# A hybrid decoder layer on one core: output projection, post-norm and gate kept in step order, summed in place, with the norm sums placed between matmuls

## The chip, the core and the metric

The kernel runs on one core of a Trainium2 chip. The metric is the device time of one execution in microseconds (us); of three runs of the kernel before the median is 534.99 (534.62 to 535.94). All stages are matmuls in fp32 accuracy: each fp32 operand is split into a high part, rounded by ScalarE (ACT), and the rest, formed by VectorE (DVE), and each product is three matmuls (high by high, low by high, high by low).

## The reference

T = D = 1024. Of the layer the last part matters here:

```
mixed = concat(ssm_out, attn_out) @ w_out          # (T, 1024)
h     = x + rms_norm(mixed, post_norm_g)           # norm over the 1024 features
gate  = sigmoid(h @ pl_w_gate + pl_b_gate)
out   = h + gate * (p @ pl_w_proj)                 # p has 256 features
```

Before it come a pre-norm, the input projection, an S5 state-space branch (`ssm_out`) and a sliding-window attention branch (`attn_out`).

## The kernel before, in words

Features lie on the 128 partitions, tokens along the free dimension, so a tile `m` of 128 output features is 128 x 1024, held in two PSUM banks of 512 columns ("halves", `HALF`). A token has two orders. In time order column t is token t. In step order a column is j * 128 + c for token 8c + j: eight steps j of 128 chunks c. The state-space branch works in step order, the attention branch in time order.

The last part of the program, from L955 on:

- The first half of the output projection (4 of 8 contraction tiles, those of the state-space branch) has been run during attention; its result stands in two tiles `mixed` in step order.
- `per_layer(m)` (L957) is `p @ pl_w_proj` for tile m: 12 matmuls from `pt` (p, transposed and split), copied out by ACT into `pls`. Tiles 0 to 2 are run ahead of the projection.
- `a_hi`, `a_lo` (L973 to L977) are the split of the attention output `q_f`, one instruction per block of 128 tokens on ACT and one on DVE. The last block comes from the last attention unit, whose DVE instruction L799 (`q_f<-ps,z_att`) gates it.
- The loop L981 runs the second half of the output projection, 24 matmuls a tile. DVE adds each half to `mixed` (L993) and writes `total` in time order, which makes the operand `mixed` strided; ACT squares it (L994); DVE gathers `sumsq` (L998, and by halves for the last tile, L996).
- `over_partitions` (L125) sums `sumsq` over the partitions with eight one-column matmuls (each shows as two). `row_rstd` (L132) makes the reciprocal root of it with 12 small DVE instructions and spreads it over the partitions with eight transposes (L151) and two ACT copies (`postb`).
- `make_h(k)` (L1007) forms tile k of h: DVE scales (L1015) and adds x (L1016), ACT and DVE split (L1018, L1019).
- The gate: tiles 0, 1, 2 are run together over k (18 matmuls per k, L1053 to L1058), as h comes; tiles 3 to 7 after that, one by one. The weights of tile 2 go into a tile `w_2` of their own (L1047 to L1051), loaded once `make_h(1)` has run.

Order: a scheduler sets the order on ACT, DVE and the DMA queue (SP) by priorities and modelled times; PE's order in the blocks `manual_schedule` is as written. Every engine runs its own instructions strictly in that order. Space: `t16` gives seven slots of 16 KB per partition, `t4` four of 4 KB, `w_st` two for weights as they land, `w_hi` and `w_lo` four each for the split. A new tile in a slot waits until the old one was read for the last time. `run` on the host lays out the inputs; that is not part of the time.

Of the kernel before, what the change touches and what calls it, by code (L numbers as in the profile page):

```python
# [20 lines left out]
P = 128  # L21
# [30 lines left out]


def layer_kernel(
    tc, x_in, xT, pT, w_in, w_glu, w_out, w_gate, w_proj, vecs, sinks,
    lam_re, lam_im, log_step, bc, ssm_d, out,
):
    nc = tc.nc
# [2 lines left out]
    with ExitStack() as top:  # L61
# [13 lines left out]
        def t16(shape, dt, name):  # L75
            return mp.tile(shape, dt, name=name, tag="t16", bufs=7)

        def t4(shape, dt, name):
            return mp.tile(shape, dt, name=name, tag="t4", bufs=BUFS["t4"])
# [26 lines left out]
                w.append((hi, lo))  # L106
            return w

        def product(ps, w, act, ks, first=True, last=True):

            ah, al = act
            for n, (kw, ka) in enumerate(ks):
                wh, wl = (t[:, kw % 4, :] for t in w[kw // 4])
                f, l = first and n == 0, last and n == len(ks) - 1
                for h, o in enumerate(ps):
                    PE.matmul(o, lhsT=wh, rhs=ah(ka, h), start=f, stop=False)  # L116
                for h, o in enumerate(ps):
                    PE.matmul(o, lhsT=wh, rhs=al(ka, h), start=False, stop=False)  # L118
                for h, o in enumerate(ps):
                    PE.matmul(o, lhsT=wl, rhs=ah(ka, h), start=False, stop=l)  # L120

        def by_half(tiles, n=4):
            return lambda k, h: tiles[k // n][:, k % n, h * HALF : (h + 1) * HALF]

        def over_partitions(sumsq):  # L125
            ps = bank("w")
            for t in range(8):
                PE.matmul(ps[:, t : t + 1], lhsT=sumsq[:, t * P : (t + 1) * P],
                          rhs=ones_col, start=True, stop=True)
            return ps[:, 0:8]  # L130

        def row_rstd(sums, name, between):  # L132
# [819 lines left out]
                n += 1  # L952
        run_pieces(n, end)

        pls = []  # L955

        def per_layer(m):  # L957
            w = load_split(w_proj[m], 2)
            ps = psum_pair("tab" if m % 3 == 1 else "mm")
            product(ps, w, (by_half([pt[:, 0]]), by_half([pt[:, 1]])), [(0, 0), (1, 1)])  # L960
# [10 lines left out]
        for m in range(3):  # L971
            per_layer(m)
        a_hi = t16([P, 4, T], F32R, "a_hi")  # L973
        a_lo = t16([P, 4, T], F32R, "a_lo")
        for b in range(NB):
            qs = slice(b * P, (b + 1) * P)
            split_to(a_hi[:, :, qs], a_lo[:, :, qs], q_f[:, :, qs])  # L977
        total = [t16([P, 4, T], F32, "total") for _ in range(2)]
        sumsq = t4([P, T], F32, "sumsq2")
        aact = (by_half([a_hi]), by_half([a_lo]))  # L980
        for m in range(KT):  # L981
            w = load_split(w_out[m][:, 4:KT], 4)
            ps = psum_pair("tab" if m % 3 == 1 else "mm")
            product(ps, w, aact, [(k, k) for k in range(4)])
            sq = sumsq if m == 0 else t4([P, T], F32, "sq2")
            for h, o in enumerate(ps):
                hs = slice(h * HALF, (h + 1) * HALF)
                mix = total[m // 4][:, m % 4, hs]

                def chunks(t):  # L990
                    return t.rearrange("p (c j) -> p c j", j=CH)
                steps = mixed[m // 4][:, m % 4, :].rearrange("p (j c) -> p c j", j=CH)[:, 64 * h : 64 * h + 64, :]
# [12 lines left out]
        lows = []

        def make_h(k):  # L1007
            x2 = t4([P, T], F32, "x2")
            nc.sync.dma_start(out=x2, in_=xT[k * P : (k + 1) * P, :])
# [20 lines left out]
            nc.sync.dma_start(out=out[m * P : (m + 1) * P, hs], in_=t)  # L1030

        with tc.manual_schedule(engines={mybir.EngineType.PE}):
            def some(lo, hi):
                for m in range(lo, hi):
                    per_layer(m)
# [7 lines left out]
            w_first = [load_split(w_gate[m], KT) for m in range(2)]  # L1043
            with tc.high_priority(offset=2 * AHEAD):
                made = make_h(1)

            w2 = t16([P, 2, KT, P], F32R, "w_2")  # L1047
            w_first.append([(w2[:, 0, 4 * i : 4 * i + 4], w2[:, 1, 4 * i : 4 * i + 4]) for i in range(2)])
            with tc.issue_after(made.ins):
                for i in range(2):  # L1050
                    load_part(*w_first[2][i], w_gate[2], slice(4 * i, 4 * i + 4))  # L1051
# [79 lines left out]
```

## Time and profile before

| | us |
|---|---|
| median of three runs | 534.99 |
| the profiled execution | 535.14 |
| its span | 533.4 |
| PE busy in the span | 517.3 (97%) |
| DVE, ACT busy | 379.8, 214.2 |

PE is the engine of matmuls, PEld its weight loads, SPq the issue of DMAs by SyncE. "Busy" of PE counts any running matmul, a one-column one too; "idle before" in brackets is the time in which the engine waited, and what released it. The 1.7 us between the span and the time of the execution lie around the program.

### The profile page before, as it was taken

Reading aid. Unit: us, or ns where it says so; the run is one execution under the profiler, and the core shown is the slowest. Engines: PE = TensorE matmul, PEld = TensorE weight load, DVE = VectorE, ACT = ScalarE, POOL = GpSimd, SP = SyncE. Lnnn points to the kernel's source line nnn. Section 1 sums busy time; section 2 is a strip of 40 time slices with the busy share of each in tenths; the row PEclk is TensorE's granted clock in tenths of the full one; section 3 lists DMA queues with packets and bytes.
Section 4 is the critical chain, followed back from the end, with each engine's and each line's share of the span. In section 5 each row is a group of like instructions: output and inputs, shape, how many; then the busy total and the mean of one; then the engine's idle time right before and its main releaser. Section 6 shows DMA issues by size and latency. Waiting matters only on the chain.

```text
span 533.4 us, 7319 instructions
## 1 busy us (share of the span) xinstructions
PE 517.3 (97%) x2472; PEld 410.4 (77%) x2472; DVE 379.8 (71%) x864; ACT 214.2 (40%) x443; POOL 8.6 (2%) x37
## 2 busy tenths in 40 slices
PE   7999999999999999999899999999999998999996
PEld 5888887888888888886445767777788886888886
DVE  4778997989889898654699667666467679736232
ACT  5676120311122322233775656667332373223121
POOL 1000000000000000010000000000000000000000
PEclk9999999899999999999999999999999989999999
DMA  7961638344443434559575122101111165124112
GB/s 268 372 233 60 217 93 196 95 128 121 122 117 97 120 95 117 176 145 252 169 213 190 47 60 60 30 22 39 61 49 30 67 218 174 65 80 172 66 39 79
DMA packets 48053, 66.10 MB, mean 124 GB/s; under 512 B 10128, under 2 KB 25232, under 8 KB 48016
## 3 DMA queue, kind: packets, MB, share of 16 engines
q1 hardware_dynamic: 46736, 63.54, 38.6%
q10 hardware_dynamic: 1280, 2.10, 1.5%
q8 instruction: 19, 0.31, 0.3%
q14 instruction: 18, 0.15, 0.1%
HBM read 44.12 MB, written 11.01 MB: 103 GB/s over the span
## 4 chain that ended last, share of the span: by engine, by line
PE 80%; DVE 9%; DMA 7%; SPq 1%; issue 1%; ACT 1%; ACTq 0%; DVEq 0%
PE ps_mm L118 18%; PE ps_mm L116 18%; PE ps_mm L120 18%; PE ps_tab L120 4%; PE ps_tab L116 4%; PE ps_tab L118 4%; PE ps_mm L866 3%; DMA y_all<-y_dr 2%; PE ps_w L794 2%; PE ps_y L794 2%; PE ps_tab L737 1%; PE ps_tab L738 1%; PE ps_y L594 1%; PE ps_w L520 1%; DVE e L314 1%
## 5 line engine op out<-in xcount | busy, mean ns | idle before, releaser
L88 ACT ACTIVATE w_hi<-w_st 128x512 fp32r<-128x512 f32 (+1 forms) x68 | 41.2, 606 | 132.3 <-PE ps_mm L118 80.6
L116 PE MATMUL ps_mm<-x_hi,w_hi 128*128 128x512 f32 x272 | 86.3, 399 | 2.3 <-ACT x_hi L178 1.7
L118 PE MATMUL ps_mm<-x_lo,w_hi 128*128 128x512 f32 x272 | 87.7, 399 | 0.0
L120 PE MATMUL ps_mm<-x_hi,w_lo 128*128 128x512 f32 x272 | 87.4, 398 | 0.0
L89 DVE TENSOR_TENSOR w_lo<-w_st,w_hi 128x512 fp32r<-128x512 f32 (+1 forms) x68 | 44.8, 659 | 38.7 <-ACT w_hi L88 32.4
L116 PEld LDWEIGHTS ps_mm<-x_hi,w_hi 128*128 128x128 f32 x272 | 51.3, 191 | 13.6 <-ACT x_hi L178 2.2
L118 PEld LDWEIGHTS ps_mm<-x_lo,w_hi 128*128 128x128 f32 x272 | 51.6, 191 | 10.5
L120 PEld LDWEIGHTS ps_mm<-x_hi,w_lo 128*128 128x128 f32 x272 | 51.2, 191 | 10.2 <-DVE w_lo L89 0.3
L118 PE MATMUL ps_mm<-h_lo,w_hi 128*128 128x512 f32 (+1 forms) x96 | 30.8, 380 | 0.0
L116 PE MATMUL ps_mm<-h_hi,w_hi 128*128 128x512 f32 (+1 forms) x96 | 30.8, 380 | 0.0
L120 PE MATMUL ps_mm<-h_hi,w_lo 128*128 128x512 f32 (+1 forms) x96 | 30.7, 380 | 0.0
L761 ACT ACTIVATE sc<-sc,mx 128x129 f32<-128x129 f32 x64 | 25.1, 395 | 12.9 <-DVE mx L754 12.7
L866 PE MATMUL ps_mm<-y_all,w_glu 128*128 128x512 f32 x64 | 29.1, 596 | 1.2 <-DMA w_glu<-in_w_glu 1.2
L1028 DVE SCALAR_TENSOR_TENSOR o_t<-o_t,pls 128x512 f32<-128x512 f32 (+1 forms) x17 | 10.9, 658 | 20.0 <-ACT o_t L1027 20.0
L866 PEld LDWEIGHTS ps_mm<-y_all,w_glu 128*128 128x128 f32 x64 | 11.5, 190 | 13.5 <-issue 10.6
L116 PE MATMUL ps_mm<-m_hi,w_hi 128*128 128x512 f32 x64 | 21.8, 404 | 0.0
L120 PE MATMUL ps_mm<-m_hi,w_lo 128*128 128x512 f32 x64 | 21.7, 402 | 0.0
L118 PE MATMUL ps_mm<-m_lo,w_hi 128*128 128x512 f32 x64 | 21.7, 398 | 0.0
L118 PEld LDWEIGHTS ps_mm<-h_lo,w_hi 128*128 128x128 f32 x96 | 18.0, 188 | 3.5
L116 PEld LDWEIGHTS ps_mm<-h_hi,w_hi 128*128 128x128 f32 x96 | 18.0, 188 | 3.5
L120 PEld LDWEIGHTS ps_mm<-h_hi,w_lo 128*128 128x128 f32 x96 | 18.0, 188 | 3.5
L314 DVE TENSOR_TENSOR sw<-sw,si 128x512 f32<-128x512 f32 x16 | 11.1, 693 | 11.4 <-DMA sw<-s 8.4
(265 smaller groups left out, 1022.9 us busy)
## 6 DMA issues: line engine op xcount, KB each, us to landing
w_st<-in_w_in SPq DMA_DIRECT2D x30, 256.0 KB
w_st<-in_w_out SPq DMA_DIRECT2D x16, 256.0 KB
w_st<-in_w_gate SPq DMA_DIRECT2D x16, 256.0 KB
x<-in_xT SPq DMA_DIRECT2D x8, 512.0 KB
out_T<-o_t SPq DMA_DIRECT2D x15, 256.0 KB
x_sq<-in_xT SPq DMA_DIRECT2D x4, 512.0 KB
x_st<-in_x SPq DMA_DIRECT2D x4, 512.0 KB
x_sq<-in_x SPq DMA_DIRECT2D x4, 512.0 KB
```

Source lines behind the costliest of these rows:

```text
L88: S.activation(hi, t, AF.Copy)
L89: V.tensor_tensor(out=lo, in0=t, in1=hi.bitcast(F32), op=ALU.subtract)
L116: PE.matmul(o, lhsT=wh, rhs=ah(ka, h), start=f, stop=False)
L118: PE.matmul(o, lhsT=wh, rhs=al(ka, h), start=False, stop=False)
L120: PE.matmul(o, lhsT=wl, rhs=ah(ka, h), start=False, stop=l)
L314: V.tensor_tensor(out=o, in0=a, in1=b, op=op)
L520: PE.matmul(ps[:, g * NC : (g + 1) * NC], lhsT=m[:, g * P : (g + 1) * P], rhs=U[:, g, :], start=True, stop=True)
L594: PE.matmul(ps[:, g * NC + 1 : (g + 1) * NC], lhsT=qt[:, g * P : (g + 1) * P], rhs=s[:, g * NC : (g + 1) * NC - 1], start=False, stop=True)
L761: S.activation(self.sc[:, m, :], self.sc[:, m, :], AF.Exp, bias=self.mx[:, m : m + 1], scale=-1.0, accum_out=self.sm[:, m : m + 1])
L794: PE.matmul(pv[64 * kv : 64 * kv + 64], lhsT=v[:, cols], rhs=p[:, 2 * kv : 2 * kv + 2, :], start=n == 0, stop=n == len(parts) - 1)
L866: PE.matmul(self.ps, lhsT=self.w[:, k, :], rhs=glu_in["y"][:, self.hf, k, :], start=k == 0, stop=k == 3)
L1028: V.scalar_tensor_tensor(out=t, in0=t, scalar=1.0, in1=pls[2 * m + h][:, a : a + n], op0=ALU.add, op1=ALU.mult)
```

## The change

- The host hands x a second time in step order (`xS`), and p in step order; the output is in step order and put back on the host.
- The output projection still runs in time order, but L1009 of the changed kernel adds PSUM to `mixed` in place, in step order: now the PSUM operand is read with a stride of eight elements (32 bytes), and `mixed` is read and written in runs of 64. The two `total` tiles are gone.
- The weights of `per_layer` 3 to 7 are loaded and split early, into a new `t16` tile `wp`.
- `w_2` (gate tile 2) is loaded and split during the output projection, ahead of tiles 0 and 1.
- `per_layer(3)` no longer stands between the projection and the norm sums. Each of the eight norm sums is followed by one matmul of `per_layer`, eight more stand ahead of the transposes, and the rest after them.

```
-        def product(ps, w, act, ks, first=True, last=True):
+        def products(ps, w, act, ks, first=True, last=True):
...
-                    PE.matmul(o, lhsT=wh, rhs=ah(ka, h), start=f, stop=False)
+                    yield PE.matmul(o, lhsT=wh, rhs=ah(ka, h), start=f, stop=False)
...
+        def product(*args, **kw):
+            for _ in products(*args, **kw):
+                pass
...
-        def over_partitions(sumsq):
+        def over_partitions(sumsq, others):
             ps = bank("w")
             for t in range(8):
                 PE.matmul(ps[:, t : t + 1], lhsT=sumsq[:, t * P : (t + 1) * P],
                           rhs=ones_col, start=True, stop=True)
+                next(others, None)
...
+        FIRST = 3
         def per_layer(m):
-            w = load_split(w_proj[m], 2)
+            if m < FIRST:
+                w = load_split(w_proj[m], 2)
+            else:
+                w = [tuple(wp[:, n, m - FIRST] for n in range(2))]
...
+        wp = t16([P, 2, KT - FIRST, 2, P], F32R, "wp")
+        for a, b in ((FIRST, 6), (6, KT)):
+            st = t4([P, b - a, 2, P], F32, "wp_st")
+            nc.sync.dma_start(out=st, in_=w_proj[a:b].rearrange("m p k n -> p m k n"))
+            split_to(wp[:, 0, a - FIRST : b - FIRST], wp[:, 1, a - FIRST : b - FIRST], st)
...
-        total = [t16([P, 4, T], F32, "total") for _ in range(2)]
...
-                V.tensor_tensor(out=chunks(mix), in0=chunks(o), in1=steps, op=ALU.add)
-                S.activation(sq[:, hs], mix, AF.Square)
+                def half(t):
+                    return t.rearrange("p (j c) -> p j c", j=CH)[:, :, 64 * h : 64 * h + 64]
+                mix = half(mixed[m // 4][:, m % 4, :])
+                V.tensor_tensor(out=mix, in0=o.rearrange("p (c j) -> p j c", j=CH), in1=mix, op=ALU.add)
+                S.activation(half(sq), mix, AF.Square)
...
+        w2 = t16([P, 2, KT, P], F32R, "w_2")
+        w2 = [(w2[:, 0, 4 * i : 4 * i + 4], w2[:, 1, 4 * i : 4 * i + 4]) for i in range(2)]
+        for i in range(2):
+            load_part(*w2[i], w_gate[2], slice(4 * i, 4 * i + 4))
+        w_first = [load_split(w_gate[m], KT) for m in range(2)] + [w2]
...
-            some(3, 4)
+            others = (s for m in range(FIRST, KT) for s in per_layer(m))
+            def some(n):
+                for _ in range(n):
+                    next(others)
             with tc.high_priority():
-                rstd2 = row_rstd(over_partitions(sumsq), "post", lambda _: some(4, 5))
-            some(5, KT)
+                rstd2 = row_rstd(over_partitions(sumsq, others), "post", lambda _: some(8))
+            for _ in others:
+                pass
```

Three places of the instruction order. First PE, from the last matmul of the output projection (`a_hi`) to the transposes (`postr`); `sumsq` are the norm sums, `pt` the products of `per_layer`. Before:

```order
L120 MATMUL ps_tab<-a_hi,w_lo 128x512 x2
L116 MATMUL ps_mm<-pt,w_hi 128x512 x2
L118 MATMUL ps_mm<-pt,w_hi 128x512 x2
L120 MATMUL ps_mm<-pt,w_lo 128x512 x2
...
L128 MATMUL ps_w<-ones_col,sumsq_3637 128x1 x8
L116 MATMUL ps_tab<-pt,w_hi 128x512 x2
...
L151 MATMUL ps_y<-ident,postr 128x128 x4
L151 MATMUL ps_w<-ident,postr 128x128 x4
```

The same place now:

```order
L120 MATMUL ps_tab<-a_hi,w_lo 128x512 x2
L133 MATMUL ps_w<-ones_col,sumsq_3644 128x1
L116 MATMUL ps_mm<-pt,wp 128x512
...
L118 MATMUL ps_mm<-pt,wp 128x512 x2
L120 MATMUL ps_mm<-pt,wp 128x512 x2
L116 MATMUL ps_tab<-pt,wp 128x512 x2
L118 MATMUL ps_tab<-pt,wp 128x512 x2
L157 MATMUL ps_y<-ident,postr 128x128 x4
L157 MATMUL ps_w<-ident,postr 128x128 x4
```

Before, 12 products stand ahead of the sums, 12 between sums and transposes, 36 after them; now none, 8 among the sums, 8 ahead of the transposes, 44 after them.

Second DVE, about the last two gates of attention (`q_f<-ps,z_att`) and the split of the attention output (`a_lo`). Before:

```order
L89 TENSOR_TENSOR a_lo<-q_f,a_hi 128x4x128 x5
L799 TENSOR_TENSOR q_f<-ps_w,z_att 128x2x128
L89 TENSOR_TENSOR a_lo<-q_f,a_hi 128x4x128 x2
L89 TENSOR_TENSOR w_lo<-w_st,w_hi 128x512
L784 TENSOR_TENSOR p_own<-ps_y,own_t 128x512
L89 TENSOR_TENSOR w_lo<-w_st,w_hi 128x512 x3
L799 TENSOR_TENSOR q_f<-ps_y,z_att 128x2x128
L89 TENSOR_TENSOR a_lo<-q_f,a_hi 128x4x128
```

Now:

```order
L89 TENSOR_TENSOR wp<-wp_st,wp 128x768
L89 TENSOR_TENSOR wp<-wp_st,wp 128x512
L89 TENSOR_TENSOR w_lo<-w_st,w_hi 128x512
L805 TENSOR_TENSOR q_f<-ps_w,z_att 128x2x128
L790 TENSOR_TENSOR p_own<-ps_y,own_t 128x512
L89 TENSOR_TENSOR w_lo<-w_st,w_hi 128x512 x2
L805 TENSOR_TENSOR q_f<-ps_y,z_att 128x2x128
L89 TENSOR_TENSOR a_lo<-q_f,a_hi 128x4x128 x7
```

Seven of the eight `a_lo` blocks have moved from before the last gate to behind it; `wp` stands where the first of them stood.

Third the DMA queue SP, where the weights of the projection end (`w_out`) and those of the gate (`w_gate`) and x (`x`) follow. Before:

```order
L94 DMA w_st<-in_w_out 128x512 x8
L94 DMA w_st<-in_w_proj 128x256 x5
L94 DMA w_st<-in_w_gate 128x512 x2
L1009 DMA x<-in_xT 128x1024
...
L94 DMA w_st<-in_w_gate 128x512
```

Now:

```order
L94 DMA w_st<-in_w_out 128x512 x8
L94 DMA w_st<-in_w_gate 128x512 x8
L1028 DMA x<-in_xS 128x1024
...
L94 DMA w_st<-in_w_gate 128x512 x3
L1049 DMA out_T<-o_t 128x512
```

All weights of the first three gate tiles, and those of the fourth, are now issued ahead of x; before, only two of eight loads were.

## Rows read from the trace of the kernel before

**Rows 1.** The page: busy time, and the chain that ended last by engine.
```profile
PE 517.3 (97%) x2472; PEld 410.4 (77%) x2472; DVE 379.8 (71%) x864; ACT 214.2 (40%) x443; POOL 8.6 (2%) x37
...
PE 80%; DVE 9%; DMA 7%; SPq 1%; issue 1%; ACT 1%; ACTq 0%; DVEq 0%
```
**Rows 2.** Stretches: us from:to, length, busy per engine (count), granted clock, DMA, GB/s.
```profile
376.40:420.09 43.69, 43.69 (x194) 36.14 (x193) 27.17 (x31) 13.92 (x24) 0.00 (x0) 1.00 0.13 39
420.09:423.13 3.04, 2.88 (x14) 2.07 (x12) 3.04 (x5) 1.76 (x5) 0.00 (x0) 1.00 0.00 0
423.13:425.07 1.94, 1.94 (x17) 1.94 (x18) 0.88 (x2) 0.94 (x2) 0.00 (x0) 1.00 0.39 141
...
426.18:429.04 2.86, 2.86 (x9) 2.07 (x7) 1.00 (x6) 0.57 (x2) 0.00 (x0) 0.52 0.90 333
...
441.34:445.11 3.77, 1.20 (x5) 0.68 (x5) 3.77 (x6) 2.29 (x3) 0.00 (x0) 1.00 0.38 117
```
**Rows 3.** Timeline of PE: start, us, line, tiles, count, [idle before <-releaser].
```profile
376.40 0.50 PE L116 MATMUL ps_mm<-a_hi,w_hi 128*128 128x512 f32 x1
...
420.09 0.62 PE L116 MATMUL ps_mm<-pt,w_hi 128*128 128x512 f32 x2
...
423.13 1.95 PE L128 MATMUL ps_w<-ones_col,sumsq 128*128 128x1 f32 x16 [0.16 <-DVE sumsq L996]
...
429.04 0.94 PE L151 MATMUL ps_y<-ident,postr 128*128 128x128 f32 x4
...
430.17 0.70 PE L116 MATMUL ps_mm<-pt,w_hi 128*128 128x512 f32 x2
...
438.46 0.61 PE L116 MATMUL ps_mm<-h_hi,w_hi 128*128 128x512 f32 x2
...
442.83 0.73 PE L116 MATMUL ps_tab<-h_hi,w 128*128 128x512 f32 x2 [1.49 <-ACT w L88]
...
445.11 0.73 PE L120 MATMUL ps_tab<-h_hi,w 128*128 128x512 f32 x2 [1.08 <-DVE w L89]
```
**Rows 4.** Timeline of DVE about the last gates of attention.
```profile
364.80 3.26 DVE L89 TENSOR_TENSOR a_lo<-q_f,a_hi 128x512 fp32r<-128x512 f32 x5 [2.57 <-ACT a_hi L88]
...
371.25 0.69 DVE L784 TENSOR_TENSOR p_own<-ps_y,own_t 128x512 f32<-128x512 f32 x1
...
376.97 0.42 DVE L799 TENSOR_TENSOR q_f<-ps_y,z_att 128x256 f32<-128x256 f32 x1
```
**Rows 5.** Timeline of ACT: the split of the last attention block.
```profile
377.42 0.63 ACT L88 ACTIVATE a_hi<-q_f 128x512 fp32r<-128x512 f32 x1 [0.62 <-DVE q_f L799]
```
**Rows 6.** Timeline of DVE from the projection's end to the norm, and the first h.
```profile
420.06 2.08 DVE L993 TENSOR_TENSOR total<-ps_tab,mixed 128x512 f32<-128x512 f32 x2 [1.45 <-PE ps_tab L120]
422.05 0.42 DVE L89 TENSOR_TENSOR w_lo<-w_st,w_hi 128x256 fp32r<-128x256 f32 x1
422.39 1.29 DVE L996 TENSOR_TENSOR sumsq<-sumsq,sq 128x512 f32<-128x512 f32 x2
...
425.11 0.17 DVE L135 TENSOR_SCALAR postv<-ps_w 128x8 f32<-128x8 f32 x1 [1.10 <-PE ps_w L128]
...
427.20 0.17 DVE L144 SCALAR_TENSOR_TENSOR postr<-poste,postr 128x8 f32<-128x8 f32 x1
...
430.69 2.62 DVE L1015 SCALAR_TENSOR_TENSOR total<-total,vec,postb 128x512 f32<-128x512 f32 x3 [0.66 <-ACT postb L153]
...
439.16 1.22 DVE L1019 TENSOR_TENSOR h_lo<-total,h_hi 128x1024 fp32r<-128x1024 f32 x1
440.30 1.28 DVE L1015 SCALAR_TENSOR_TENSOR total<-total,vec,postb 128x1024 f32<-128x1024 f32 x1
441.49 1.22 DVE L1016 TENSOR_TENSOR total<-total,x 128x1024 f32<-128x1024 f32 x1
```
**Rows 7.** One line's instructions: ns min/median/max. L993, the add with a strided operand.
```profile
L993 DVE TENSOR_TENSOR total<-ps_tab,mixed x6: 1067/1078/1089, 382.2 to 421.0; 128x512 f32<-128x512 f32 x6
```
**Rows 8.** Timeline of ACT: the weights of gate tile 2.
```profile
442.15 0.63 ACT L88 ACTIVATE w<-w_st 128x512 fp32r<-128x512 f32 x1 [2.12 <-DMA w_st<-in_w_gate]
```

More of the change, by code (lines that the diff above doesn't have):

```diff
@@ L54, in layer_kernel @@
 def layer_kernel(
[L55 removed]
+    tc, x_in, xT, xS, pT, w_in, w_glu, w_out, w_gate, w_proj, vecs, sinks,
     lam_re, lam_im, log_step, bc, ssm_d, out,
@@ L115, in product @@
                 for h, o in enumerate(ps):
-                    PE.matmul(o, lhsT=wh, rhs=ah(ka, h), start=f, stop=False)
+                    yield PE.matmul(o, lhsT=wh, rhs=ah(ka, h), start=f, stop=False)
                 for h, o in enumerate(ps):
-                    PE.matmul(o, lhsT=wh, rhs=al(ka, h), start=False, stop=False)
+                    yield PE.matmul(o, lhsT=wh, rhs=al(ka, h), start=False, stop=False)
                 for h, o in enumerate(ps):
-                    PE.matmul(o, lhsT=wl, rhs=ah(ka, h), start=False, stop=l)
+                    yield PE.matmul(o, lhsT=wl, rhs=ah(ka, h), start=False, stop=l)
+        def product(*args, **kw):
+            for _ in products(*args, **kw):
+                pass
         def by_half(tiles, n=4):
             return lambda k, h: tiles[k // n][:, k % n, h * HALF : (h + 1) * HALF]
-        def over_partitions(sumsq):
+        def over_partitions(sumsq, others):
             ps = bank("w")
@@ L955, in layer_kernel @@
         pls = []
+        FIRST = 3
         def per_layer(m):
-            w = load_split(w_proj[m], 2)
+            if m < FIRST:
+                w = load_split(w_proj[m], 2)
+            else:
+                w = [tuple(wp[:, n, m - FIRST] for n in range(2))]
             ps = psum_pair("tab" if m % 3 == 1 else "mm")
-            product(ps, w, (by_half([pt[:, 0]]), by_half([pt[:, 1]])), [(0, 0), (1, 1)])
+            yield from products(ps, w, (by_half([pt[:, 0]]), by_half([pt[:, 1]])), [(0, 0), (1, 1)])
             for o in ps:
@@ L970, in layer_kernel @@
             split_to(pt[:, 0, k, :], pt[:, 1, k, :], t)
-        for m in range(3):
-            per_layer(m)
+        for m in range(FIRST):
+            for _ in per_layer(m):
+                pass
[4 more added lines that the diff above has]
+            split_to(wp[:, 0, a - FIRST : b - FIRST], wp[:, 1, a - FIRST : b - FIRST], st)
         a_hi = t16([P, 4, T], F32R, "a_hi")
@@ L987, in layer_kernel @@
                 hs = slice(h * HALF, (h + 1) * HALF)
[L988 to L992, printed above, removed]
-                V.tensor_tensor(out=chunks(mix), in0=chunks(o), in1=steps, op=ALU.add)
-                S.activation(sq[:, hs], mix, AF.Square)
+                def half(t):
[3 more added lines that the diff above has]
+                S.activation(half(sq), mix, AF.Square)
                 if m == KT - 1:
-                    V.tensor_tensor(out=sumsq[:, hs], in0=sumsq[:, hs], in1=sq[:, hs], op=ALU.add)
+                    V.tensor_tensor(out=half(sumsq), in0=half(sumsq), in1=half(sq), op=ALU.add)
             if 0 < m < KT - 1:
                 V.tensor_tensor(out=sumsq, in0=sumsq, in1=sq, op=ALU.add)
-        mixed = total
-        h_hi = [t16([P, 4, T], F32R, f"h_hi{i}") for i in range(2)]
-        h_lo = [t16([P, 4, T], F32R, f"h_lo{i}") for i in range(2)]
+        w2 = t16([P, 2, KT, P], F32R, "w_2")
[3 more added lines that the diff above has]
+        w_first = [load_split(w_gate[m], KT) for m in range(2)] + [w2]
+        h_hi, h_lo = zip(*[[t16([P, 4, T], F32R, f"h_{n}{i}") for n in ("hi", "lo")] for i in range(2)])
         hact = (by_half(h_hi), by_half(h_lo))
@@ L1032, in layer_kernel @@
         with tc.manual_schedule(engines={mybir.EngineType.PE}):
-            def some(lo, hi):
-                for m in range(lo, hi):
-                    per_layer(m)
-            some(3, 4)
+            others = (s for m in range(FIRST, KT) for s in per_layer(m))
+            def some(n):
+                for _ in range(n):
+                    next(others)
             with tc.high_priority():
-                rstd2 = row_rstd(over_partitions(sumsq), "post", lambda _: some(4, 5))
-            some(5, KT)
+                rstd2 = row_rstd(over_partitions(sumsq, others), "post", lambda _: some(8))
+            for _ in others:
+                pass
             with tc.high_priority(offset=2 * AHEAD):
                 make_h(0)
[L1043 to L1051, printed above, removed]
+                make_h(1)
             ps_first = [psum_pair("tab" if m == 2 else "mm") for m in range(3)]
@@ L1105, with steps @@
     wo = np.concatenate([wo[:512], _pairs(wo[512:], 0)], axis=0)
+    def steps(a):
+        return c(a.reshape(-1, NC, CH).transpose(0, 2, 1).reshape(-1, T))
     def cols(a):
@@ L1129 @@
     r = run(nc, [{"in_" + n: a for n, a in ins.items()}], core_ids=[0])
-    return c(r.results[0]["out_T"].T).reshape(1, T, D)
+    return c(r.results[0]["out_T"].reshape(D, CH, NC).transpose(2, 1, 0)).reshape(1, T, D)
```

4 lines of the change are left out of this document (2 added, 2 removed).

## The prediction

> **What bounds the kernel now.** First the page: PE is busy for 517.3 of 533.4 us, and the chain that ended last lies on PE for 80% [rows 1]. Next to nothing is to be had from faster ACT, DVE or DMA as such; what counts is where PE waits, or runs slowly, and whether the change adds such places. So I then read the stretches about the end of the output projection, and the timelines of PE, DVE and ACT in them.
>
> The projection itself has no gap: 192 products in 43.69 us, from 376.40 to 420.09, are 0.2276 us each at clock 1.00 [rows 2, 3]. From its end to 445.11, where the gate runs freely, PE does 76 products (60 of `per_layer`, 16 of the gate), which at this pitch would take 17.3 us; it takes 25.0. The 7.7 us lost are, one after the other [rows 2, 3]:
>
> - 420.09 to 423.13: 12 products (2.73) cover the time in which DVE finishes `sumsq`; lost 0.31.
> - 423.13 to 425.07: the norm sums, 16 one-column matmuls, 1.94, PEld busy throughout.
> - [...]
> - 429.04 to 430.17: the transposes, 1.13; partly still at the low clock.
> - 430.17 to 438.46: 36 products in 8.29; lost 0.10.
> - 438.46 to 445.11: 16 products in 6.65; lost 3.01. Two waits for `w_2`, 1.49 and 1.08, are most of it; the split of its weights stood until 442.15 for their DMA [rows 8]. In this stretch PE was busy for only 1.20 of 3.77 us and yet the clock stayed at 1.00 [rows 2].
>
> **The change part by part**, against the profiled execution (535.14; the median of the runs, 534.99, is 0.15 lower).
>
> *Weights of gate tile 2 early.* On DVE and on the queue they now stand ahead of the norm, so both waits go, and nothing in their place: h is in time. After the scale starts, DVE needs 2.62 for the scales of h0 and h1, then two adds (1.29 and 1.22) and the 1.29 of splitting h0, 6.4 together, while PE has 44 products left after the transposes, 10.0. After that each k costs DVE 1.28 + 1.22 + 1.22 = 3.72 [rows 6] and PE 18 products, 4.10. x now comes behind all those weights on the queue, but the last of them waits only for a split that ends 2.6 after the projection's end, and the first add of x comes some 13 after it (4.0 + 2.8 + 2.3 + 1.0 + 2.6, below). Gain 3.0.
>
> *The split of the attention output.* `wp` takes a slot of 16 KB at the place where `a_lo` stood, and `a_lo` comes to lie in that of `z_att`, which the last gate reads. So seven of its blocks stand behind that gate on DVE. Before, five of them ran from 364.80 on [rows 4], beside PE's products. Now the gate ends at 377.39 and the blocks follow at (3.26 - 0.69) / 4 = 0.64 each: the fourth is done at about 377.3 + 3 x 0.64 + 0.69 = 379.9. PE can start at 376.40 with the two `a_hi` products of the first half, must wait for the others for the last `a_hi` block, 378.05 [rows 5], and for its first `a_lo` until 380.0. It then has 6 products done, which free of waits would have been so at 377.77. Loss 2.2 (2.0 to 2.4). Once past it the second half's `a_lo`, done by about 383.3, is wanted only at 387.
>
> *No products ahead of the norm sums.* Now PE stands before the first sum until DVE has both halves of `sumsq` (in step order each block of 128 columns holds chunks of both halves). DVE's row of it: two adds, 2.08; a weight split, now 128x512 instead of 128x256, 0.64 at its pitch; two `sumsq` adds, 1.29 [rows 6]. From 420.06 this ends 3.9 later, with the release 4.0 after the projection's end, with nothing on PE beside it. Before, 0.31 was lost here. Loss 3.7, if the add with its PSUM operand read at a stride takes as long as now.
>
> This the trace doesn't show. Below: a DVE instruction with a contiguous PSUM operand takes 0.69 for 512 elements [rows 4]; twice 0.38 less gives a wait of 3.2. Above: if the stride cost PSUM twice what it costs `mixed` (1.08 against 0.69 [rows 4, 7]), 1.5 each and a wait of 4.8. I take 1.08: L993 also has one strided operand and two plain ones. [...] The same adds in mid-projection cost nothing: 2.1 + 1.2 + two splits at 0.64 are 4.6 of a tile's 5.46 on PE.
>
> *Sums among products.* Before 1.94 for the sums alone. Now eight products, 1.82, stand between them. If all their weight loads hide beside products, 1.82 for both; if none, 3.76. I take 2.8, one of the two loads of each hidden: 0.97 less than now (0 to 1.9).
>
> *Between sums and transposes.* DVE's chain takes 2.3 from 425.11 to 427.37 [rows 6], PE has nine products, 2.05, so it waits 0.3; then transposes, about 1.0. Lost 1.3, against 1.24 + 1.13 = 2.37 now, if the clock holds.
>
> *The clock.* It fell after 1.94 us of sums, and it didn't after two waits of 1.49 and 1.08 with products between [rows 2, 3]. The new wait of 4.0 is longer than any of these, and one-column matmuls like those ahead of the fall follow it. I expect a fall like the one before, beside the same kind of work, and the same price, 1.2 (0, or twice that for two low stretches).
>
> *The rest.* Strided runs of 64 in the squares, other layouts of x, p and the output cost nothing: ACT has half of the time free and transfers are as large as before. The gate from 445.11 on is the same.
>
> Sum: 2.2 + 3.7 - 0.97 + (1.3 + 1.2 - 2.37 = 0.1) - 3.0 = +2.1. That is 537.2 on the profiled 535.14, and 537.1 on the median; I say 537.2.
>
> **Rivals.**
>
> *The clock holds and the loads hide.* Alternating keeps PE at its upper level, and the sums run in the shadow of products: 1.2 and about 0.9 less, so 0.0 to +0.1, 535.0: not slower. For it: the clock outlived 2.57 us of waiting in 3.77 [rows 2]. Against: that was broken up by products, the new wait isn't. It decides when the granted clock of the first products after the sums reads 1.00. [...] In the rows PEld is busy for all of the 1.94 us of the sums, where no products were there to hide it.
>
> *The PSUM stride is dear.* At 1.5 us an add the wait before the sums is 4.8, and a second low stretch of the clock costs another 1.2: 537.2 + 0.8 + 1.2 = 539.2. For it: L993's strided operand costs it half as much again as a row without one. Against: the strided operand only changes place.
>
> *The early weights come late all the same.* Their splits share two landing buffers with those of the projection; should the last of them fall behind the norm, up to 3.0 are not gained: 540.2. Against: the split stands ahead of the last three tiles' adds on DVE.
>
> *Faster.* PE's wait before the sums is given back when the two new waits are both at their lower ends and the clock holds: 2.0 + (3.2 - 0.3) - 1.9 - 1.1 - 3.0 = -1.1, 534.0; more than this the removed losses don't hold, as 7.7 is all there is and transposes, the first `a_lo` and `sumsq` must stay.
>
> **How the numbers follow.** Forecast 0.52, clock held 0.27, dear stride 0.12, late weights 0.04, faster (by something not in these rows beyond the -1.1) 0.05. 0.3% is 1.6 us, about what a measurement of this kernel tells from no change: same is 533.4 to 536.6. The forecast's own range is 535.9 to 538.9, about a sixth of it below 536.6. Slower: 0.44 + 0.16 = 0.60; same: 0.27 + 0.08 = 0.35; faster 0.05. The range reaches from the held clock's lower part to the dear stride, 534.4 to 539.8.
>
> **What would show it.** In the profile of the changed kernel: PE idle for 1.2 and 0.9 about 377 to 380, released by the last `a_hi` and by an `a_lo`; the last projection matmul near 422.3; PE idle for 3.2 to 4.8 before L133, released by `sumsq`; L1009 at 1.08; a low clock after it; no wait for `w_2` in the gate. I am wrong if the first `a_lo` is there by 378, if the wait before the sums is under 2.5, or if the gate waits for h, x or weights.

## The result, and the profile after

| kernel | median of runs, us | from to | ratio to the kernel before, 95% interval | profiled execution, span, us |
|---|---|---|---|---|
| before, beside the first runs after | 535.47 (6) | 534.62 to 536.54 | | 535.14, 533.4 |
| after | 539.78 (6) | 538.62 to 543.6 | 1.0071 [1.0044, 1.0099] | 538.62, 536.9 |
| after, a second time, beside other runs of before | 539.55 (12) | 536.82 to 541.1 | 1.0058 [1.0033, 1.0083] | 540.61, 538.8 |

The number in brackets counts the runs. By the ratios the change makes the kernel slower by 3.8 and 3.1 us; the first two medians lie 4.3 apart. The page of the profile after has nearly the shares of [rows 1]; they don't tell where the time went:

```profile
PE 519.3 (97%) x2472; PEld 412.1 (77%) x2472; DVE 372.9 (69%) x861; ACT 213.2 (40%) x440; POOL 8.6 (2%) x37
...
PE 83%; DVE 8%; DMA 5%; ACT 2%; SPq 1%; issue 1%; DVEq 0%; ACTq 0%
```

PE is busy for 2 us more with as many matmuls as before. The timeline of PE in the profile after answers to [rows 3]:

```profile
375.92 0.65 PE L800 MATMUL ps_y<-p,v_f 128*64 128x256 f32 x4
376.40 0.60 PE L800 MATMUL ps_y<-p_own,v_step 128*64 128x256 f32 x4
376.93 0.50 PE L116 MATMUL ps_mm<-a_hi,w_hi 128*128 128x512 f32 x1
...
378.19 0.50 PE L116 MATMUL ps_mm<-a_hi,w_hi 128*128 128x512 f32 x1 [0.53 <-ACT a_hi L88]
...
380.06 0.50 PE L118 MATMUL ps_mm<-a_lo,w_hi 128*128 128x512 f32 x1 [0.67 <-DVE a_lo L89]
...
421.88 0.61 PE L120 MATMUL ps_tab<-a_hi,w_lo 128*128 128x512 f32 x2
425.46 0.38 PE L133 MATMUL ps_w<-ones_col,sumsq 128*128 128x1 f32 x2 [2.96 <-DVE sumsq L1012]
425.70 0.48 PE L116 MATMUL ps_mm<-pt,wp 128*128 128x512 f32 x1
426.02 0.28 PE L133 MATMUL ps_w<-ones_col,sumsq 128*128 128x1 f32 x2
426.15 0.48 PE L116 MATMUL ps_mm<-pt,wp 128*128 128x512 f32 x1
...
427.99 0.77 PE L120 MATMUL ps_mm<-pt,wp 128*128 128x512 f32 x1
428.57 0.42 PE L133 MATMUL ps_w<-ones_col,sumsq 128*128 128x1 f32 x2
428.85 0.77 PE L120 MATMUL ps_mm<-pt,wp 128*128 128x512 f32 x1
...
434.22 0.60 PE L157 MATMUL ps_y<-ident,postr 128*128 128x128 f32 x4
...
445.11 0.61 PE L116 MATMUL ps_mm<-h_hi,w_hi 128*128 128x512 f32 x2
...
447.83 0.61 PE L116 MATMUL ps_tab<-h_hi,w 128*128 128x512 f32 x2
```

There are two short waits at the projection's start, one of 2.96 us ahead of the first norm sum, and none at all in the gate, where [rows 3] had 1.49 and 1.08. (A bracket counts from the shown end of the product before, which overlaps the next in an unbroken row; by the starts each of these waits costs PE 0.2 to 0.3 us more than its bracket.) A sum and a product follow each other at a pitch of 0.45 us at 426 and of 0.86 at 428. The stretches say why (columns as in [rows 2]):

```profile
422.33:425.46 3.13, 0.17 (x2) 0.00 (x1) 3.07 (x5) 1.55 (x3) 0.00 (x0) 1.00 0.06 7
425.46:426.92 1.46, 1.46 (x9) 1.34 (x10) 0.00 (x0) 0.00 (x0) 0.00 (x0) 1.00 1.00 330
426.92:433.50 6.58, 6.58 (x22) 5.61 (x21) 1.91 (x12) 0.85 (x2) 0.00 (x0) 0.51 0.56 202
435.01:445.11 10.10, 10.10 (x47) 8.35 (x46) 9.58 (x11) 6.32 (x12) 0.00 (x0) 1.00 0.32 104
```

In the wait, 3.13 us from the point where the next product could have started, DVE is busy for 3.07 us and ACT for 1.55. Behind it the granted clock is 0.51 for 6.58 us (6.8 us at 0.50 by half-microsecond stretches); before it was 0.52 for 2.86 us in [rows 2] (3.4 us at 0.50).

To compare executions, the tail, from V on, is cut at points that each timeline shows: V, the start of the last attention unit's values (375.92 above); P, the end of the projection's last product; S, the first sum; T, the first transpose; G, the gate's first product; E, the end of the span, which is given to 0.1 us, so that the columns to E are good to 0.05. "Low" is the time at a granted clock of 0.50 between 420 and 470, summed from half-microsecond stretches: each of them reads 0.50, 1.00 or, at an edge, a value between, which is counted in part.

| trace | V | V to P | P to S | S to T | T to G | G to E | V to E | low |
|---|---|---|---|---|---|---|---|---|
| before | 375.38 | 44.87 | 2.88 | 5.91 | 9.42 | 94.94 | 158.02 | 3.4 |
| before, second trace | 378.37 | 44.87 | 2.87 | 6.01 | 9.32 | 94.96 | 158.03 | 3.4 |
| after | 375.92 | 46.57 | 2.97 | 8.76 | 10.89 | 91.79 | 160.98 | 6.8 |
| after, second trace | 376.15 | 46.61 | 2.96 | 10.08 | 11.15 | 91.85 | 162.65 | 10.2 |
| twelve products of cover | 377.17 | 46.61 | 2.95 | 5.90 | 8.19 | 91.78 | 155.43 | 0 |
| twelve idle products | 376.29 | 46.61 | 2.95 | 5.99 | 10.88 | 91.78 | 158.21 | 0 |
| a first | 377.09 | 44.86 | 2.96 | 10.19 | 10.88 | 91.82 | 160.71 | 10.2 |
| both | 376.18 | 44.88 | 2.95 | 5.91 | 8.22 | 91.76 | 153.72 | 0 |
| both, sums in a row | 377.75 | 44.87 | 2.96 | 4.29 | 10.03 | 91.80 | 153.95 | 0 |
| both, sixteen products | 375.13 | 44.87 | 3.47 | 5.80 | 7.31 | 91.82 | 153.27 | 0 |
| before, sums alternating | 376.44 | 44.86 | 2.88 | 6.74 | 8.22 | 94.76 | 157.46 | 0 |
| w_2 late | 376.20 | 46.61 | 2.96 | 8.78 | 10.89 | 91.76 | 161.00 | 6.8 |
| without wp | 376.83 | 44.87 | 2.69 | 8.77 | 10.89 | 92.75 | 159.97 | 6.8 |
| without wp, w_2 late | 377.40 | 44.86 | 2.69 | 8.75 | 10.89 | 98.81 | 166.00 | 13.7 |

V itself differs by 3.0 us between two executions of the kernel before; the 0.54 of it between the first traces of before and after are no effect that can be told from this scatter. The tail, cut off from it, is 2.96 us longer after (4.62 in the second traces). Of the 60 per-layer products before, 12 stand in P to S, 12 in S to T, 36 in T to G; after, 0, 16 and 44. With the products that moved counted at 0.228 each, the 2.96 of the first traces are: late `a_lo` +1.70; ahead of the sums +0.09 and 12 products (2.73) pushed behind, +2.82; sums to transposes 2.85 - 4 x 0.228 = +1.94; transposes to gate 1.47 - 8 x 0.228 = -0.35; gate -3.15.

### The profile page after: what moved, and what is told of

Same layout as the page of the kernel before. It is cut to its first block, busy times and chain, and to the rows that moved or that the text cites. A ratio compares the mean times of both kernels' runs of the same rounds, so it can differ in the third digit from the quotient of the medians.

```text
span 536.9 us, 7299 instructions
## 1 busy us (share of the span) xinstructions
PE 519.3 (97%) x2472; PEld 412.1 (77%) x2472; DVE 372.9 (69%) x861; ACT 213.2 (40%) x440; POOL 8.6 (2%) x37
## 4 chain that ended last, share of the span: by engine, by line
PE 83%; DVE 8%; DMA 5%; ACT 2%; SPq 1%; issue 1%; DVEq 0%; ACTq 0%
PE ps_mm L118 18%; PE ps_mm L120 18%; PE ps_mm L116 18%; PE ps_tab L116 4%; PE ps_tab L118 4%; PE ps_tab L120 4%; PE ps_mm L872 3%; PE ps_w L800 2%; PE ps_y L800 2%; PE ps_tab L743 1%; DMA y_all<-y_dr 1%; PE ps_tab L744 1%; PE ps_w L526 1%; PE ps_y L600 1%; PE ps_y L598 1%; DVE e L320 1%
## 5 line engine op out<-in xcount | busy, mean ns | idle before, releaser
L88 ACT ACTIVATE w_hi<-w_st 128x512 fp32r<-128x512 f32 (+1 forms) x63 | 39.2, 622 | 128.7 <-PE ps_mm L118 86.0
L89 DVE TENSOR_TENSOR w_lo<-w_st,w_hi 128x512 fp32r<-128x512 f32 (+1 forms) x63 | 42.3, 672 | 36.9 <-ACT w_hi L88 32.1
L120 PEld LDWEIGHTS ps_mm<-x_hi,w_lo 128*128 128x128 f32 x272 | 51.1, 191 | 10.2 <-DVE w_lo L89 0.3
L872 PEld LDWEIGHTS ps_mm<-y_all,w_glu 128*128 128x128 f32 x64 | 11.4, 190 | 13.7 <-issue 10.3
L743 PE MATMUL ps_tab<-kk,bq 128*128 128x256 f32 (+1 forms) x64 | 17.8, 303 | 1.8 <-ACT sc L746 1.8
```

The source lines that it names most:

```text
L88: S.activation(hi, t, AF.Copy)
L89: V.tensor_tensor(out=lo, in0=t, in1=hi.bitcast(F32), op=ALU.subtract)
L120: yield PE.matmul(o, lhsT=wl, rhs=ah(ka, h), start=False, stop=l)
L743: PE.matmul(o, lhsT=l, rhs=kk_hi[:, kv, k0 : k0 + wk], start=True, stop=False)
L872: PE.matmul(self.ps, lhsT=self.w[:, k, :], rhs=glu_in["y"][:, self.hf, k, :], start=k == 0, stop=k == 3)
```

## The experiments

Theory A: PE's uncovered wait ahead of the sums costs twice, once as idle time and once by the low clock that follows it; beside it stands the late `a_lo`. Rival B: the alternation of one-column sums with products keeps the clock low. Rival C: the loss is elsewhere.

**Cover.** Products that are due anyway run in the wait: twelve of the first tile in `wp`, ahead of the sums (`last` is the projection's last product):

```
+            with tc.issue_after(last.ins):
+                some(12)
             with tc.high_priority():
                 rstd2 = row_rstd(over_partitions(sumsq, others), "post", ...)
```

> The changed kernel with twelve products of the per-layer term (its fourth tile) set between the end of the output projection and the first norm sum; the sums still alternate with the eight products that follow. Theory A (TensorE's uncovered wait of 3.13 us ahead of the sums, and the low clock that follows it, are where most of the time was lost): the twelve products run inside that wait, so the first sum waits 0.3 to 0.5 us and 2.7 us are won; the stretch at a granted clock near 0.5 becomes as short as in the kernel before (3.4 us instead of 7.3), which wins another 1.9 us. Together 4.6 us: some 535.2 us, ratio to the kernel before 0.999. Rival B (it is the alternation of one-column sums with products that holds the clock down): the low stretch stays at some 7 us, only the 2.7 us are won: 537.1 us, ratio 1.003. Rival C (neither counts, the loss lies upstream of the last gate): no change, 539.8 us, ratio 1.007.

Measured: 533.8 us, ratio 0.9956 [0.9929, 0.9984], tail 155.43. Stretches of this run, columns as above, up to the first sum and from there to the transposes:

```profile
425.88:426.73 0.85, 0.61 (x4) 0.19 (x2) 0.79 (x2) 0.43 (x1) 0.00 (x0) 1.00 0.20 48
426.73:432.63 5.90, 5.75 (x32) 4.72 (x33) 1.91 (x12) 1.72 (x4) 0.00 (x0) 1.00 0.85 285
```

The clock stays at 1.00 with the alternation as it was: B falls, C too. More is won than A said (5.55 us of tail against 4.6), as no low stretch is left at all.

**Idle products.** The two halves of A, taken apart: twelve extra products into a bank that nothing reads, in the same place, so that the sums and everything behind stay where they were.

```
+            idle = bank("y")
+            with tc.issue_after(last.ins):
+                for _ in range(12):
+                    PE.matmul(idle, lhsT=wp[:, 0, 0, 0], rhs=pt[:, 0, 0, 0:HALF], ...)
```

> The changed kernel with twelve extra 512-column products that nothing reads, set between the end of the projection and the first norm sum (extra work, 12 x 0.228 = 2.7 us of it; nothing of the kernel's own is moved or left out). The sums can start no earlier than before, so the order and the 3.1 us ahead of them stay; only TensorE is busy in them. Theory A in two halves (the uncovered wait is paid once in itself and once more through the clock that falls behind it): the granted clock stays near 1.0 through the sums, the stretch of 7 us at 0.50 goes, and with it some 3.2 us: ratio to the kernel before 1.001 instead of 1.007. Rival (the clock falls for another reason in this stretch, as the sums or the DMA's traffic behind them): low stretch as in the changed kernel, ratio 1.007, or 1.008 where the extra work delays the sums by 0.4 us.

Measured: 535.77 us, ratio 0.9988 [0.9961, 1.0015]. PE's timeline and two stretches of this run:

```profile
422.73 2.88 PE L1062 MATMUL ps_y<-pt,wp 128*128 128x512 f32 x12
425.85 0.38 PE L134 MATMUL ps_w<-ones_col,sumsq 128*128 128x1 f32 x2 [0.24 <-DVE sumsq L1013]
```
```profile
425.85:429.58 3.73, 3.73 (x24) 3.40 (x25) 0.14 (x1) 0.00 (x0) 0.00 (x0) 1.00 0.94 316
429.58:431.84 2.26, 2.00 (x10) 1.35 (x8) 1.77 (x12) 1.07 (x2) 0.00 (x0) 1.00 0.65 252
```

P to S is as long as after (2.95), S to T falls from 8.76 to 5.99, and the tail by 2.77. Work that computes nothing makes the changed kernel faster: the clock alone is worth 2.8 us in this trace (against the second trace of after 4.4), and the idle time as much again: the run with cover has a tail 2.78 us shorter than this one. DMA moves 316 GB/s behind the first sum here, with the clock at 1.00, so its traffic (330 and 202 after) doesn't lower the clock by itself.

**a first.** `a_hi`, `a_lo` and their split are moved ahead of `wp`'s allocation, load and split; no other line changes.

> The changed kernel with one edit: the attention output's two halves a_hi and a_lo are allocated and split ahead of the per-layer weights wp, so that a_lo takes a free room again and wp takes the one that the gate's operand z_att leaves. Theory (the late split of a_lo costs 2.2 us): the split of a_lo goes on behind each gate, the product that reads it first waits for nothing or at most 0.3 us, and six products of the projection are done some 2 us earlier than at 380.06 us; wp is split only after 377 us but not read before 425 us, so nothing is paid for it: 537.6 us, ratio to the kernel before 1.004. Rival (what a_lo's wait held up is made good by the weights' buffers further on, or the wait only changes its name): no change, 539.8 us, ratio 1.007. The wait of 3.1 us ahead of the sums stays in both.

Measured: 538.2 us, ratio 1.0022 [0.9989, 1.0055]. PE's timeline at the projection's start, and the two stretches ahead of and behind the first sum:

```profile
377.09 0.65 PE L800 MATMUL ps_y<-p,v_f 128*64 128x256 f32 x4
...
378.10 0.50 PE L116 MATMUL ps_mm<-a_hi,w_hi 128*128 128x512 f32 x1
378.44 0.40 PE L118 MATMUL ps_mm<-a_lo,w_hi 128*128 128x512 f32 x1
```
```profile
421.79:424.91 3.12, 0.17 (x1) 0.00 (x0) 3.07 (x5) 1.55 (x3) 0.00 (x0) 0.95 0.05 5
424.91:435.10 10.19, 10.19 (x32) 8.67 (x33) 1.91 (x12) 1.07 (x2) 0.00 (x0) 0.51 0.51 178
```

The first `a_lo` is there at once, and V to P is 44.86, as before: 1.70 us, where 2.2 were expected. In this execution most of it went into a low stretch of 10.2 us, which the second trace of after has as well: against that one its tail is 1.94 shorter, against the first only 0.27.

**Both**, and both with the sums in a row (the `next(others, None)` in `over_partitions` left out):

> Both edits: a_hi and a_lo ahead of wp, and twelve products of the per-layer term between the projection and the first sum. If both losses are what theory A says and they add: 539.8 less 4.6 less 2.2 = 533.0 us, ratio to the kernel before 0.995, faster than either kernel, since the early third gate tile's weights (3.0 us) are then kept without the two prices. Rival B (the alternation itself holds the clock down for 7 us): 539.8 less 2.7 less 2.2 = 534.9 us, ratio 0.999. Rival C: 537.6 us or more.

> As the run with both edits, but the eight sums stand in a row, followed by eight products, the transposes and the rest, so that only the alternation differs. Theory A: the trace of the changed kernel shows 0.455 us for a pair of a sum and a product at full clock, 0.228 more than a product alone, so the sums' weight loads are not hidden by the alternation, and in a row (0.24 us each before) they cost the same; the clock does as the wait ahead of it says. So the same time as with alternation within 0.5 us: 533 us, ratio to the kernel before 0.995. The recorded prediction's own step (eight sums among products add 1.0 us to them instead of 1.94): 1.0 us slower than alternating. Rival B (alternation holds the clock down): 1.9 us faster than alternating.

Measured: both 531.5 us, ratio 0.9923 [0.9897, 0.995]; in a row 532.86 us, 0.9959 [0.9932, 0.9986]. The gains add: the tail is 153.72, 7.3 us under that of after. In a row it is 153.95; the intervals of the ratios overlap, so the difference of the medians isn't settled, but the tails differ by 0.23 us, not by the 1.0 that the prediction gave the alternation. A row of eight sums took as much beside products as by itself, but for this 0.23.

**Both, with sixteen products** of cover, `some(16)`:

> As the run with a_hi and a_lo first and twelve products of cover, but with sixteen. The trace of that run has 0.40 us of idle time between the last covering product and the first sum; four more products take 0.91 us, so the first sum comes 0.5 us later and waits for nothing: 0.4 us won, ratio to the kernel before 0.9915 instead of 0.992, with the clock at 1.0 throughout, as there. Rival (0.5 us later sums delay rstd, h and the gate by as much): no difference or 0.1 us lost, ratio 0.992 to 0.993.

Measured: 530.22 us, ratio 0.99 [0.9868, 0.9933], the lowest ratio here. PE goes from the cover into the sums without a wait:

```profile
423.01 0.62 PE L118 MATMUL ps_tab<-pt,wp 128*128 128x512 f32 x2
423.47 0.28 PE L134 MATMUL ps_w<-ones_col,sumsq 128*128 128x1 f32 x2
423.60 0.48 PE L120 MATMUL ps_tab<-pt,wp 128*128 128x512 f32 x1
```

The tail is 0.45 us shorter than with twelve, as expected; that is in the traces, while the intervals of the two ratios overlap.

**The alternation on the kernel before**: twelve products, the eight sums alternating with eight products, then eight more; all else as before.

> The kernel before with one part of the change: the eight sums alternate with the first eight products of the next per-layer tile, and eight more stand between the sums and the transposes (twelve before); twelve stay ahead of the sums, and w_2, a_lo and the sum in total stay as before. Theory A: a sum beside a product costs 0.228 us, as much as in a row (0.24), so nothing is won or lost, and the clock does as it does in the kernel before: ratio 1.000 within 0.001. The recorded prediction's step (sums hidden in part among products): 1.0 us won, ratio 0.998. Rival B (alternation holds the clock down for 7 us instead of 3.4): 1.9 us lost, ratio 1.0035.

Measured: 536.1 us, ratio 1.0001 [0.9976, 1.0026]. The edit is worth nothing in the runs. In its trace no clock falls, but a wait stands in the place: PE's transposes, and DVE's row ahead of them:

```profile
430.92 0.65 PE L157 MATMUL ps_y<-ident,postr 128*128 128x128 f32 x4 [0.99 <-DVE postr L150]
```
```profile
428.85 0.17 DVE L148 TENSOR_TENSOR poste<-postr 128x8 f32<-128x8 f32 x1
429.29 0.69 DVE L89 TENSOR_TENSOR w_lo<-w_st,w_hi 128x512 fp32r<-128x512 f32 x1 [0.27 <-ACT w_hi L88]
429.90 0.16 DVE L149 TENSOR_TENSOR poste<-poste,postv 128x8 f32<-128x8 f32 x1
```

A weight split that waits for ACT fell into the middle of the norm's chain and lengthened it: 3.09 us, where the kernel before has 2.26. So this run doesn't price the alternation alone; the two runs with both edits do.

**Who removed the gate's waits.** Three runs: `w_2` loaded behind the second h again; `wp` undone (each tile's weights by the staging buffer, the first gate tiles' loads behind the products, as before) with `w_2` early; both undone.

```
-        w2 = t16([P, 2, KT, P], F32R, "w_2")
...
-            load_part(*w2[i], w_gate[2], slice(4 * i, 4 * i + 4))
...
+                made = make_h(1)
...
+            with tc.issue_after(made.ins):
+                for i in range(2):
+                    load_part(*w_first[2][i], w_gate[2], slice(4 * i, 4 * i + 4))
```
```
-            if m < FIRST:
-                w = load_split(w_proj[m], 2)
-            else:
-                w = [tuple(wp[:, n, m - FIRST] for n in range(2))]
+            w = load_split(w_proj[m], 2)
...
-        wp = t16([P, 2, KT - FIRST, 2, P], F32R, "wp")
...
-        w_first = [load_split(w_gate[m], KT) for m in range(2)] + [w2]
...
+            w_first = [load_split(w_gate[m], KT) for m in range(2)] + [w2]
+            with tc.high_priority(offset=2 * AHEAD):
                 make_h(1)
```

> The changed kernel with one part undone: the third gate tile's weights w_2 are again loaded and split behind the second tile of h, as in the kernel before. The recorded prediction's term (early weights are worth 3.0 us): waits of 1.49 and 1.08 us at the third gate tile return, ratio to the kernel before 1.0125. Counted from the changed kernel's own trace: between the transposes' end and the gate there are 44 products, 8 more than before, 1.8 us, so the late weights have 1.8 us more cover and only 0.8 to 1.4 us of wait return: ratio 1.009. Rival (early weights are worth nothing in the new order): no wait, ratio 1.007.

> The changed kernel with the per-layer weights of tiles 3 to 7 loaded tile by tile through the staging buffer again, as in the kernel before, instead of kept in wp; w_2 stays early, the first two gate tiles' loads stand behind the products as in the kernel before, and a_lo has a free room. Question: which part of the change removed the third gate tile's waits of 1.49 and 1.08 us. Theory P (its place in the order did): no wait at the third gate tile; a_lo no longer waits, some 2 us won against the changed kernel: ratio to the kernel before 1.003. Theory S (the staging buffers freed by wp did, so that all gate loads leave the queue early): with w_2 ahead of the per-layer loads there is no wait on w_2 either, but the first and second gate tiles' loads, late again, may show waits of up to 1 us: ratio 1.005. The wait of 3.1 us ahead of the sums and the low clock behind it stay in both.

> As the run without wp, and w_2 late as well, so that all loads of this stretch stand in the order of the kernel before. With w_2 late but wp kept, no wait returned, since the gate's loads were issued from 397 to 425 us; here the five per-layer loads stand before them in the queue again. Theory S: the waits at the third gate tile return, 1.5 to 2.6 us, so the ratio to the kernel before is 1.006 to 1.008 with a_lo's 2 us won. Rival (the 44 products between transposes and gate, eight more than before, are cover enough): no wait, ratio 1.003 as the run without wp.

Measured: `w_2` late 540.1 us, 1.0078 [1.0049, 1.0107]; without `wp` 537.48, 1.0027 [1.0003, 1.0051]; both undone 543.68, 1.0147 [1.0112, 1.0183]. PE's timeline about the third gate tile (`ps_tab`), in this order:

```profile
448.16 0.62 PE L116 MATMUL ps_tab<-h_hi,w 128*128 128x512 f32 x2
```
```profile
447.79 0.50 PE L116 MATMUL ps_tab<-h_hi,w 128*128 128x512 f32 x1 [0.29 <-ACT pls L971]
```
```profile
447.97 0.73 PE L120 MATMUL ps_mm<-h_hi,w_lo 128*128 128x512 f32 x2 [0.95 <-DVE w_lo L89]
451.24 1.22 PE L116 MATMUL ps_tab<-h_hi,w 128*128 128x512 f32 x2 [2.54 <-ACT w L88]
...
453.78 1.22 PE L120 MATMUL ps_tab<-h_hi,w 128*128 128x512 f32 x2 [0.46 <-DVE w L89]
```

Against the first two expectations for a late `w_2`, it waits for nothing while `wp` is there: the tail is 161.00 against 160.98. The queue says why (SP's issues: start, time they span, count), with `w_2` late and `wp` kept, and then with both undone:

```profile
397.38 27.49 SPq L94 DMA_DIRECT2D w_st<-in_w_gate  x6
```
```profile
396.79 21.82 SPq L94 DMA_DIRECT2D w_st<-in_w_proj  x5
423.73 10.10 SPq L94 DMA_DIRECT2D w_st<-in_w_gate  x2
```

With both undone, five per-layer loads stand in the landing buffers ahead of the gate's. Either edit gets `w_2` past them, the second adds nothing to the first. So `wp`, which took the room of `a_lo` for 1.70 us, gives back only 0.96 in the gate (92.75 against 91.79); without it, and with the first two tiles' loads late again, the changed kernel's tail is 1.0 shorter, though the intervals of the two ratios to the same runs of before (1.0027 and 1.0058) overlap. With both undone the tail is 6.0 longer than without `wp` alone, more than expected: 3.95 of waits, of which 0.29 were there without `wp` alone, and a second low stretch behind the idle 2.54:

```profile
449.67:456.32 6.65, 4.62 (x10) 3.23 (x11) 6.65 (x7) 2.68 (x4) 0.00 (x0) 0.51 0.74 250
```

**Both kernels a second time.**

> A second look at the kernel before, for the granted clock alone. Its first trace shows 0.50 to 0.65 from 426 to 430 us, just behind the sums, while runs with the same twelve products ahead of the sums held 1.0 there. If the low stretch belongs to this kernel's order: low again for 3 to 4 us at the same place. If it comes and goes from one execution to the next: 1.0 throughout, or low elsewhere.

> The changed kernel once more, on the chip and in the rounds of the runs beside it: ratio to the kernel before 1.007 as measured first. Its trace, if the low clock belongs to the wait of 3.1 us: about 0.50 for 6 to 10 us from within 2 us of the first sum; if it comes and goes: 1.0 throughout.

Measured: before 538.11 us in its one run; after as in the first table. The low stretches, of before and of after:

```profile
426.11:428.05 1.94, 1.94 (x17) 1.94 (x18) 0.89 (x2) 0.94 (x2) 0.00 (x0) 1.00 0.38 141
429.29:432.70 3.41, 3.41 (x12) 2.63 (x11) 1.17 (x7) 1.14 (x3) 0.00 (x0) 0.51 0.75 293
```
```profile
422.77:425.72 2.95, 0.00 (x0) 0.00 (x0) 2.90 (x5) 1.38 (x3) 0.00 (x0) 1.00 0.07 12
425.72:435.80 10.08, 10.08 (x33) 8.43 (x33) 1.91 (x12) 1.07 (x2) 0.00 (x0) 0.52 0.53 178
```

Both are there again at their places, and the longer one differs from execution to execution. What lowers the clock for 3.4 us in the kernel before stays open: the run with both edits and its sums in a row has nearly the same order there, a wait of 0.24 us ahead of it (before 0.16 and 0.15), and no low clock.

## Why the prediction was right, and where not

The forecast was +2.1 us, 537.2; it came to +3.8, and +3.1 the second time. The median, 539.78, is inside the range by 0.02 us only, beside a median of before 0.48 above the 534.99 from which the range was counted. The mechanism is the one forecast, but two terms were too large and two too small: in the tail, late `a_lo` and the wait came out 1.4 us lower than reckoned, the way from the first sum to the gate 2.5 higher (+1.59 where -0.87 stood). That the sum came as near as it did is partly luck. So is that the time lies by the 539.2 of the rival of the dear stride: that stride cost nothing, and the low clock took its place.

- *Late `a_lo`*, 2.2: 1.70 (V to P), with the wait where it was put. (The first `a_lo` product stands at 380.06, for which 380.0 was said, but V had come 0.54 later, so that agreement is chance.) The size was off because the last gate came 0.46 us sooner after the values than before (its end 377.47 - 375.92 against 377.39 - 375.38, [rows 4]): a split of weights that DVE did just ahead of it now stands behind it, at 381.73. DVE before (first line) and after:

```profile
376.36 0.69 DVE L89 TENSOR_TENSOR w_lo<-w_st,w_hi 128x512 fp32r<-128x512 f32 x1 [1.00 <-ACT w_hi L88]
```
```profile
377.05 0.42 DVE L805 TENSOR_TENSOR q_f<-ps_y,z_att 128x256 f32<-128x256 f32 x1 [2.66 <-PE ps_y L800]
377.51 4.30 DVE L89 TENSOR_TENSOR a_lo<-q_f,a_hi 128x512 fp32r<-128x512 f32 x7
```

- *No products ahead of the sums*, 3.7 with a wait of 4.0: the wait is 3.13, just under the lower bound of 3.2, the loss 2.8. The step that failed is the duration of the add with its PSUM operand at a stride, taken as 1.08 after L993 [rows 7]:

```profile
L1009 DVE TENSOR_TENSOR mixed<-ps_mm,mixed x10: 681/684/692, 382.9 to 417.5; 128x512 f32<-128x512 f32 x10
L1009 DVE TENSOR_TENSOR mixed<-ps_tab,mixed x6: 680/692/692, 385.4 to 422.9; 128x512 f32<-128x512 f32 x6
```

  It takes 0.68 to 0.69, no more than the plain 0.69 of [rows 4], and with that the rival of the dear stride falls. For PSUM the 1.08 was the author's estimate: the trace before shows that time with the stride on `mixed` alone, and no run shows it for an operand in PSUM.
- *Sums among products*, 2.8 for both, 0.97 won: 3.64 at a granted clock of 1.00 (eight pairs at 0.455; in the run with idle products the stretch of all eight is 3.73), where a row of sums and eight products take 1.94 + 1.82 = 3.76, so next to nothing is won. A sum costs 0.228 us beside a product, 0.24 in a row. PEld is busy for 3.40 of 3.73 us there (idle products, first stretch), with 25 loads to 24 matmuls: each sum has loads of its own for one column of work. That one of two loads hides beside a product was the author's estimate; no run shows it.
- *The clock*, one low stretch like the one before at the same price, no net cost: the fall came, but for 6.8 and 10.2 us instead of 3.4. By the run with idle products that is 2.8 us in the first trace (8.76 against 5.99), where 1.2 had been reckoned: 12 products took 3.97 us from 425.07 to 429.04, 1.24 more than at 0.2276 each, with the granted clock at 0.52 for the last 2.86 us [rows 2, 3] (0.70 in the transposes behind them, 429.04 to 430.17). This is the step that failed most: the prediction says of the new wait that it "is longer than any of these", and still took the price of the fall from one that followed no long wait. The rival of the clock that holds falls by all six traces with the bare wait: behind it the granted clock is 0.50 for 6.8 or 10.2 us in each.
- *Between sums and transposes*: PE doesn't wait for `postr` (DVE has it at 432.99, the transposes start at 434.22), because at the low clock PE's work takes longer (S to T is 8.76 us, with idle products and the clock at 1.00 it is 5.99); 0.3 had been charged. With the clock up, as with idle products, PE does wait there, for 0.26.
- *Early weights*, -3.0: -3.15 (G to E). The size was right. The early place alone gives 2.19 of it (94.94 against 92.75, without `wp`), but `wp` alone gives all of it (91.76, `w_2` late), which the prediction didn't see. The rival of weights that come late all the same falls: there is no wait. The prediction charged 2.2 for `wp`'s room and looked for what `wp` brings in another line.

That the two prices are what makes the change slow is shown by a kernel that keeps the change and takes back two decisions in it: with `a` first and cover ahead of the sums it is faster than the kernel before, 0.9923 with twelve products and 0.99 with sixteen.

## What to carry to other kernels

Here idle time on PE ahead of the sums was paid twice, in itself and by the clock behind it (2.78 and 2.77 us of the tail). Work that is due anyway belongs into such a wait, not behind it; a test with products that compute nothing tells the two prices apart. When a change frees room, ask which tile gets which slot: the one that is split beside running work needs the free one, and the one that is read late can have the slot that comes free late. When two edits each remove the same wait, undo both before crediting either.

## What was not expected of the hardware

- In the tail the granted clock fell after idle pieces of 2.54 us, 2.69 and 2.96 between products, in six traces of five kernels, each time to 0.50, for 6.8 or 10.2 us; after idle pieces of 0.99, 1.49 and 1.70 it stayed at 1.00. The length of the piece alone doesn't decide it: earlier in the run with both edits and its sums in a row PE is idle for 2.78 us and the clock stays at 1.00 (below), and earlier in the first trace of after the clock is 0.50 from 95.9 to 99.3, behind an idle piece of only 1.23 us. What else decides it stays open.

```profile
271.71 3.67 PE L872 MATMUL ps_mm<-y_all,w_glu 128*128 128x512 f32 x8 [2.78 <-DMA w_glu<-in_w_glu]
```
```profile
271.71:285.00 13.29, 13.29 (x43) 6.57 (x44) 10.37 (x25) 8.30 (x22) 0.59 (x1) 1.00 0.60 174
```

- A DVE add that reads PSUM with 32 bytes between neighbours took 0.684 us for 512 elements (L1009), a contiguous one 0.69 (L784 [rows 4]); with the stride on an SBUF operand read besides PSUM it had taken 1.08 (L993 [rows 7]).
- A norm sum (two one-column matmuls in the trace) cost 0.228 us even between 512-column products: 0.455 for a sum and a product, 0.2276 for a product alone.
